# Contrast adjustment of 48 image planes: another cut of the first tile, and the weights by memsets

## The chip, the cores and the metric

One NeuronCore of a Trainium2 chip runs the kernel. The metric is the device time of one execution in microseconds; smaller is better. The other numbers come from one execution that was recorded by the hardware profiler: every instruction with its start and duration on its engine (TensorE is PE, VectorE is DVE, ScalarE is ACT, GpSimd is POOL, SyncE is SP), and every packet that the core's 16 DMA engines moved.

## The reference

```python
def setup_inputs():
    batch, c, h, w = 16, 3, 512, 512
    ...
        "factor": np.float32(1.5),
...
def reference(x: np.ndarray, factor: np.float32) -> np.ndarray:
    mean = np.mean(x, axis=(2, 3), keepdims=True)
    return np.clip(mean + factor * (x - mean), 0, 1).astype(np.float32)
```

There are 16 x 3 = 48 planes of 512 x 512 float32 numbers, 50.33 MB in all. Each plane is pulled away from its own mean by the factor 1.5 and clipped to 0 to 1. A plane can only be written once all of it has been read. All 50.33 MB are read once and written once.

## The kernel before

The numbers are laid out as rows of 16384 (64 KB). A plane is 16 rows; a tile is 128 rows, one per partition, so 8 planes and 8 MB; there are 6 tiles. A ring of three tiles (192 KB in each partition) holds the data. A tile is changed in place and stored from where it was loaded, so the load of tile t + 3 into a slot waits until the same half of tile t has been stored.

SP issues all loads (`load`, line 84) and ACT all stores (`store`, line 87). The two queues share the 16 DMA engines. Each engine executes its own instructions in the order of the program; nothing is reordered.

For every tile, `add` (line 89) makes the row sums: VectorE adds the first columns of each piece (line 94, `tensor_reduce`), and ScalarE the last 3840 (line 98, an activation that copies into `junk` and accumulates). The tile is one piece, except the first and the last, which are added in two halves of 8192 columns. TensorE then multiplies the sums by `blockw` (line 105): a matrix of 128 x 128 with the number (1 - factor) / 262144 where two rows belong to the same plane and zero elsewhere. The result, `shift`, is the mean times (1 - factor), on each row of the plane. `clip` (line 110) makes the output with two VectorE instructions: times the factor plus the shift (line 112), then maximum with 0 and minimum with 1 (line 115).

`blockw` is made by GpSimd (POOL) at the start: a memset (line 66) and two affine selects (lines 68 and 72), which set to zero what lies outside the blocks of 16 x 16 on the diagonal.

Three constants cut the tiles by columns:

```python
FIRST = ((0, 2048), (2048, HALF), (HALF, ROW))
HALVES = ((0, HALF), (HALF, ROW))
WHOLE = ((0, ROW),)
```

In bytes per row FIRST is 8, 24 and 32 KB, that is 1, 3 and 4 MB of a tile. Tile 0 is loaded in two transfers: 8 KB and 56 KB (lines 120 and 121). It is added in halves, and clipped and stored by the three pieces of FIRST, each stored as soon as it is clipped. The other tiles are loaded by halves. Tiles 1 to 3 are clipped whole and stored by halves, tile 4 is clipped and stored whole, tile 5 is clipped and stored half by half. After each tile's stores the loop issues the loads of the tile three further on.

Of the kernel before, what the change touches and what calls it, by code (L numbers as in the profile page):

```python
# [1 line left out]

# [4 lines left out]


P = 128  # L10
ROW = 16384
HALF = ROW // 2
BUFS = 3

ACT = 3840

FIRST = ((0, 2048), (2048, HALF), (HALF, ROW))
HALVES = ((0, HALF), (HALF, ROW))
WHOLE = ((0, ROW),)


@with_exitstack
def kernel(
    ctx: ExitStack,
    tc: tile.TileContext,
    x: bass.AP,
    factor: float,
    out: bass.AP,
):

    nc = tc.nc
    f32 = mybir.dt.float32
    Alu = mybir.AluOpType
    Act = mybir.ActivationFunctionType

    B, C, H, W = x.shape  # L40
    n_img, n_pix = B * C, H * W
    rows = n_pix // ROW
    n_tiles = n_img * rows // P
    assert rows * ROW == n_pix and n_tiles * P == n_img * rows

    factor = float(factor)
    wconst = (1.0 - factor) / float(n_pix)

    x_f = x.rearrange("b c h w -> (b c h w)")
    out_f = out.rearrange("b c h w -> (b c h w)")  # L50

    def dram(ap, t, c0, c1):
        return bass.AP(tensor=ap.tensor, offset=t * P * ROW + c0, ap=[[ROW, P], [1, c1 - c0]])

    consts = ctx.enter_context(tc.tile_pool(name="consts", bufs=1))
    xpool = ctx.enter_context(tc.tile_pool(name="xpool", bufs=1))
    small = ctx.enter_context(tc.tile_pool(name="small", bufs=1))
    psum = ctx.enter_context(tc.tile_pool(name="psum", bufs=1, space=bass.MemoryType.PSUM))

    sums = small.tile([P, 4 * n_tiles], f32, name="sums")  # L60
    junk = small.tile([P, ACT], f32, name="junk")
    bias = psum.tile([P, n_tiles], f32, name="bias")


    blockw = consts.tile([P, P], f32, name="blockw")
    nc.gpsimd.memset(blockw, wconst)  # L66
    v = blockw.rearrange("p (g j) -> p g j", j=rows)
    nc.gpsimd.affine_select(  # L68
        out=v, in_=v, pattern=[[-rows, P // rows], [0, rows]], compare_op=Alu.is_ge,
        fill=0.0, base=0, channel_multiplier=1,  # L70
    )
    nc.gpsimd.affine_select(  # L72
        out=v, in_=v, pattern=[[rows, P // rows], [0, rows]], compare_op=Alu.is_ge,
        fill=0.0, base=rows - 1, channel_multiplier=-1,
    )

    ring = xpool.tile([P, BUFS * ROW], f32, name="ring")

    def cols(t, c0, c1):
        a = t % BUFS * ROW  # L80
        return ring[:, a + c0 : a + c1]

    def load(t, c0, c1):
        nc.sync.dma_start(out=cols(t, c0, c1), in_=dram(x_f, t, c0, c1))  # L84

    def store(t, c0, c1):
        nc.scalar.dma_start(out=dram(out_f, t, c0, c1), in_=cols(t, c0, c1))

    def add(t, pieces):

        parts = []
        for c0, c1 in pieces:
            k = 4 * t + len(parts)
            nc.vector.tensor_reduce(  # L94
                out=sums[:, k : k + 1], in_=cols(t, c0, c1 - ACT), axis=mybir.AxisListType.X,
                op=Alu.add,
            )
            nc.scalar.activation(  # L98
                out=junk, in_=cols(t, c1 - ACT, c1), func=Act.Copy,
                accum_out=sums[:, k + 1 : k + 2],  # L100
            )
            parts = [k + 1, *parts, k]
        shift = bias[:, t : t + 1]
        for i, k in enumerate(parts):
            nc.tensor.matmul(  # L105
                shift, blockw, sums[:, k : k + 1], start=i == 0, stop=i == len(parts) - 1
            )
        return shift

    def clip(t, shift, c0, c1):  # L110
        part = cols(t, c0, c1)
        nc.vector.tensor_scalar(  # L112
            out=part, in0=part, scalar1=factor, scalar2=shift, op0=Alu.mult, op1=Alu.add
        )
        nc.vector.tensor_scalar(  # L115
            out=part, in0=part, scalar1=0.0, scalar2=1.0, op0=Alu.max, op1=Alu.min
        )

    with tc.manual_schedule():
        load(0, *FIRST[0])  # L120
        load(0, FIRST[0][1], ROW)
        for t in range(1, BUFS):
            for c0, c1 in HALVES:
                load(t, c0, c1)
        for t in range(n_tiles):
            last = t == n_tiles - 1
            shift = add(t, HALVES if t == 0 or last else WHOLE)

            pieces = FIRST if t == 0 else WHOLE if t == n_tiles - 2 else HALVES
            if t == 0 or last:  # L130
                for c0, c1 in pieces:
                    clip(t, shift, c0, c1)
                    store(t, c0, c1)
            else:
                clip(t, shift, 0, ROW)
                for c0, c1 in pieces:
                    store(t, c0, c1)
            if t + BUFS < n_tiles:
                for c0, c1 in HALVES:
                    load(t + BUFS, c0, c1)  # L140


# [1 line left out]
_INS = ['x', 'factor']  # L144
_OUTS = [((16, 3, 512, 512), 'float32')]

_NUMBERS = {'factor': 1.5}


# [26 lines left out]
```

## Time and profile before

| what | us |
|---|---|
| median of 3 runs (238.91 to 239.1) | 238.98 |
| the profiled execution | 239.31 |
| its span, first to last instruction | 237.6 |
| VectorE busy | 176.8 |
| ScalarE busy | 29.3 |
| TensorE busy | 8.6 |
| GpSimd busy | 1.1 |
| last load lands | 191.48 |
| issues of the two last stores | 206.07, 214.93 |

The profile's page gives busy times by engine, the DMA engines' share in 40 slices and the two queues (q1 carries the loads, q10 the stores). A window's row has its limits and length, then busy time and number of instructions for TensorE, its weight loads, VectorE, ScalarE and GpSimd, then TensorE's granted clock, the busy share of the DMA engines and the GB/s. A row of the timeline has start, duration, engine, line, operation and shapes; in brackets stand the idle time before it and what ended that. A row of the chain of waits has start, duration and what the time is put down to.

### The profile page before, as it was taken

How to read it: one execution, taken by the hardware profiler on the slowest of the kernel's cores; microseconds unless marked ns; L12 is line 12 of the kernel's file. 1: busy time of each engine (PE TensorE's matmuls, PEld its weight loads, DVE VectorE, ACT ScalarE, POOL GpSimd, SP SyncE). 2: the span in 40 equal slices, each digit the busy share in tenths (PEclk: the TensorE clock that was granted, in tenths of full speed). 3: DMA queues.
4: the chain of work that ended last, by engine and by line, in shares of the span. 5: the costliest groups of instructions: out<-in, count | busy, mean ns of one | idle time of the engine just before them, and what ended most of it. 6: DMA issues, size and time to landing. Idle time of an engine off the chain costs nothing.

```text
span 237.6 us, 220 instructions
## 1 busy us (share of the span) xinstructions
PE 8.6 (4%) x32; PEld 7.7 (3%) x32; DVE 176.8 (74%) x26; ACT 29.3 (12%) x17; POOL 1.1 (0%) x7
## 2 busy tenths in 40 slices
PE   0000020000000000000000000000000011000000
PEld 0000020000000000000000000000000011000000
DVE  0002989999899999899898995299999778991000
ACT  2002900041000050000500000230000550000000
POOL 1000000000000000000000000000000000000000
DMA  8997999999999999999999999999999999899996
GB/s 331 463 463 331 441 441 396 418 400 443 417 476 414 414 419 441 441 436 441 441 441 441 436 408 419 419 441 441 436 441 441 441 441 502 386 397 397 441 441 265
DMA packets 3456, 100.66 MB, mean 424 GB/s; under 512 B 384, under 2 KB 384, under 8 KB 384
## 3 DMA queue, kind: packets, MB, share of 16 engines
q1 hardware_dynamic: 1728, 50.33, 49.6%
q10 hardware_dynamic: 1728, 50.33, 49.1%
HBM read 50.33 MB, written 50.33 MB: 424 GB/s over the span
## 4 chain that ended last, share of the span: by engine, by line
DVE 39%; DMA 34%; another core or an unknown queue 8%; issue 6%; PE 2%; ACT 1%; SPq 0%; DVEq 0%; ACTq 0%
DMA ring<-in_x_dram 19%; DVE sums L94 15%; DVE ring L112 15%; DMA out_dram<-ring 14%; DVE ring L115 9%; PE bias L105 2%; ACT junk L98 1%; SPq L84 0%; DVEq L112 0%; DVEq L94 0%; ACTq L98 0%
## 5 line engine op out<-in xcount | busy, mean ns | idle before, releaser
L94 DVE TENSOR_REDUCE sums<-ring 128x1 f32<-128x4352 f32 (+1 forms) x8 | 71.5, 8949 | 33.2 <-DMA ring<-in_x_dram 33.2
L112 DVE TENSOR_SCALAR ring<-ring,bias 128x16384 f32<-128x16384 f32 (+3 forms) x9 | 53.2, 5911 | 4.6 <-PE bias L105 4.6
L115 DVE TENSOR_SCALAR ring<-ring 128x16384 f32<-128x16384 f32 (+3 forms) x9 | 52.6, 5849 | 0.3
L98 ACT ACTIVATE junk<-ring 128x3840 f32<-128x3840 f32 x8 | 27.2, 3403 | 165.0 <-DMA ring<-in_x_dram 86.5
L105 PE MATMUL bias<-sums,blockw 128*128 128x1 f32 x32 | 8.6, 358 | 188.4 <-ACT junk L98 152.8
L105 PEld LDWEIGHTS bias<-sums,blockw 128*128 128x128 f32 x32 | 7.7, 319 | 189.2 <-ACT junk L98 123.8
L98 ACT ACTIVATION_READ_ACCUMULATOR junk<-ring 128x1 f32 x8 | 1.5, 187 | 0.0
L98 ACT ACT_TABLE_LOAD x1 | 1.3, 1283 | 0.8 <-PEq L157 0.8
L68 POOL TENSOR_SCALAR_AFFINE_SELECT blockw<-blockw 128x128 f32<-128x128 f32 x1 | 0.3, 345 | 0.1
L72 POOL TENSOR_SCALAR_AFFINE_SELECT blockw<-blockw 128x128 f32<-128x128 f32 x1 | 0.3, 339 | 0.1
L66 POOL MEMSET blockw<- 128x128 f32 x1 | 0.2, 206 | 0.3 <-POOLq L157 0.3
L157 POOL MEMSET const-bfloat16-1.0<- 128x1 bf16 x1 | 0.1, 102 | 0.0
L157 POOL MEMSET const-uint8-127<- 128x1 uint8 x1 | 0.1, 102 | 0.0
L157 POOL MEMSET const-float32-0.0<- 128x1 f32 x1 | 0.1, 99 | 0.3 <-issue 0.3
L157 POOL MEMSET const-float32-1.0<- 128x1 f32 x1 | 0.1, 99 | 0.0
## 6 DMA issues: line engine op xcount, KB each, us to landing
ring<-in_x_dram SPq DMA_DIRECT2D x10, 4096.0 KB, 24.8
out_dram<-ring ACTq DMA_DIRECT2D x9, 4096.0 KB, 38.7
ring<-in_x_dram SPq DMA_DIRECT2D x1, 7168.0 KB, 21.0
out_dram<-ring ACTq DMA_DIRECT2D x1, 3072.0 KB, 28.1
ring<-in_x_dram SPq DMA_DIRECT2D x1, 1024.0 KB, 4.5
out_dram<-ring ACTq DMA_DIRECT2D x1, 1024.0 KB, 16.8
out_dram<-ring ACTq DMA_DIRECT2D x1, 33.1
```

The source lines that it names most:

```text
L66: nc.gpsimd.memset(blockw, wconst)
L68: nc.gpsimd.affine_select(out=v, in_=v, pattern=[[-rows, P // rows], [0, rows]], compare_op=Alu.is_ge, fill=0.0, base=0, channel_multiplier=1,
L72: nc.gpsimd.affine_select(out=v, in_=v, pattern=[[rows, P // rows], [0, rows]], compare_op=Alu.is_ge, fill=0.0, base=rows - 1, channel_mul ...
L94: nc.vector.tensor_reduce(out=sums[:, k : k + 1], in_=cols(t, c0, c1 - ACT), axis=mybir.AxisListType.X, op=Alu.add,)
L98: nc.scalar.activation(out=junk, in_=cols(t, c1 - ACT, c1), func=Act.Copy, accum_out=sums[:, k + 1 : k + 2],)
L105: nc.tensor.matmul(shift, blockw, sums[:, k : k + 1], start=i == 0, stop=i == len(parts) - 1)
L112: nc.vector.tensor_scalar(out=part, in0=part, scalar1=factor, scalar2=shift, op0=Alu.mult, op1=Alu.add)
L115: nc.vector.tensor_scalar(out=part, in0=part, scalar1=0.0, scalar2=1.0, op0=Alu.max, op1=Alu.min)
L157: nc = _bacc.Bacc("TRN2", target_bir_lowering=False, num_devices=1)
```

## The change

The first tile is loaded by the three pieces of FIRST (8, 24 and 32 KB per row) instead of by two (8 and 56 KB). It is clipped and stored by halves (32 KB per row) instead of by the three pieces. It is still added in halves.

The weights are made by memsets alone: one over the whole matrix with zero; then, in each band of 32 rows, the second 16 columns of all 32 rows with the weight, the upper 16 rows of these columns with zero again, and the upper left 16 x 16 block with the weight. That makes 13 memsets. The matrix is the same.

```diff
+BAND = 32
...
-    nc.gpsimd.memset(blockw, wconst)
-    v = blockw.rearrange("p (g j) -> p g j", j=rows)
-    nc.gpsimd.affine_select(
-        out=v, in_=v, pattern=[[-rows, P // rows], [0, rows]], compare_op=Alu.is_ge,
-        fill=0.0, base=0, channel_multiplier=1,
-    )
-    nc.gpsimd.affine_select(
-        out=v, in_=v, pattern=[[rows, P // rows], [0, rows]], compare_op=Alu.is_ge,
-        fill=0.0, base=rows - 1, channel_multiplier=-1,
-    )
+    nc.gpsimd.memset(blockw, 0.0)
+    for a in range(0, P, BAND):
+        m = a + rows
+        nc.gpsimd.memset(blockw[a : a + BAND, m : a + BAND], wconst)
+        nc.gpsimd.memset(blockw[a:m, m : a + BAND], 0.0)
+        nc.gpsimd.memset(blockw[a:m, a:m], wconst)
...
-        load(0, *FIRST[0])
-        load(0, FIRST[0][1], ROW)
+        for c0, c1 in FIRST:
+            load(0, c0, c1)
...
-            pieces = FIRST if t == 0 else WHOLE if t == n_tiles - 2 else HALVES
+            pieces = WHOLE if t == n_tiles - 2 else HALVES
```

More of the change, by code (lines that the diff above doesn't have):

```diff
@@ L62 @@
     bias = psum.tile([P, n_tiles], f32, name="bias")
+    assert 2 * rows == BAND
     blockw = consts.tile([P, P], f32, name="blockw")
-    nc.gpsimd.memset(blockw, wconst)
-    v = blockw.rearrange("p (g j) -> p g j", j=rows)
-    nc.gpsimd.affine_select(
-        out=v, in_=v, pattern=[[-rows, P // rows], [0, rows]], compare_op=Alu.is_ge,
-        fill=0.0, base=0, channel_multiplier=1,
-    )
-    nc.gpsimd.affine_select(
-        out=v, in_=v, pattern=[[rows, P // rows], [0, rows]], compare_op=Alu.is_ge,
-        fill=0.0, base=rows - 1, channel_multiplier=-1,
-    )
+    nc.gpsimd.memset(blockw, 0.0)
[4 more added lines that the diff above has]
+        nc.gpsimd.memset(blockw[a:m, a:m], wconst)
     ring = xpool.tile([P, BUFS * ROW], f32, name="ring")
```

## The prediction

> **What bounds the kernel now.** I read the page first: the slices of the DMA engines and the two queues.
>
> ```profile
> span 237.6 us, 220 instructions
> DMA  8997999999999999999999999999999999899996
> q1 hardware_dynamic: 1728, 50.33, 49.6%
> q10 hardware_dynamic: 1728, 50.33, 49.1%
> ```
>
> Queue 1 (SP's loads) and queue 10 (ACT's stores) together hold the 16 DMA engines for 98.7% of the span. VectorE, the busiest compute engine, has 74%. Next the sums over stretches; the last two columns are the DMA share and GB/s (a packet counts where it starts).
>
> ```profile
> 3.00:35.00 32.00, 2.00 (x8) 1.86 (x8) 11.95 (x5) 7.00 (x4) 0.00 (x0) 1.00 1.02 440
> 35.00:42.00 7.00, 0.00 (x0) 0.00 (x0) 6.97 (x3) 0.00 (x0) 0.00 (x0) 1.00 0.96 370
> 69.00:192.00 123.00, 3.52 (x12) 3.01 (x12) 109.78 (x13) 14.43 (x9) 0.00 (x0) 1.00 1.00 431
> 192.00:236.40 44.40, 1.87 (x8) 1.78 (x8) 21.93 (x5) 3.06 (x2) 0.00 (x0) 1.00 0.98 424
> ```
>
> Loads alone (first row), loads beside stores (third) and stores alone (fourth) move at the same rate. Only around 35 to 42 us is less moved. The packet records (one per row of a transfer; a transfer of 128 rows gives each engine 8) say what that is. Packets of 8, 24, 32, 56 and 64 KB take 0.309, 0.912, 1.2135, 2.119 and 2.418 us: per KB nearly the same. So 100.66 MB need 3072 x 1.2135 / 16 = 233.0 us. The first packet starts at 1.80 and the last ends at 236.40, 1.17 before the end. Slow packets add 0.36 us per engine in the first 5 us, 0.70 at 34.8 to 41.3 (32 KB loads of 1.3 to 1.6 us, around the first store) and 0.27 at 50.1 to 52.7 (where the 8 KB store ends and the 24 KB one begins). Semaphore writes add 0.22. The sum 1.80 + 233.0 + 0.36 + 0.97 + 0.22 + 1.17 = 237.5 is the span: the engines never run dry.
>
> The chain of waits blames VectorE (39%) as much as DMA (34%); with the queues full, that is only who released what. For the change, the timeline of the first tile and of the last store, and the end of the chain:
>
> ```profile
> 22.26 3.40 ACT L98 ACTIVATE junk<-ring 128x3840 f32<-128x3840 f32 x1 [20.18 <-DMA ring<-in_x_dram]
> 22.34 9.28 DVE L94 TENSOR_REDUCE sums<-ring 128x1 f32<-128x4352 f32 x2 [22.34 <-DMA ring<-in_x_dram]
> 31.67 0.59 PE L105 MATMUL bias<-sums,blockw 128*128 128x1 f32 x2 [0.83 <-DVE sums L94]
> 32.30 1.29 DVE L112 TENSOR_SCALAR ring<-ring,bias 128x2048 f32<-128x2048 f32 x1 [0.68 <-PE bias L105]
> 34.88 15.93 ACTq L87 DMA_DIRECT2D out_dram<-ring  x3
> 206.07 9.20 ACTq L87 DMA_DIRECT2D out_dram<-ring  x2
> ```
>
> ```profile
> 166.63 24.85 DMA ring<-in_x_dram
> 191.56 3.50 ACT junk L98 x2
> 195.11 1.88 PE bias L105 x8
> 197.09 4.50 DVE ring L112
> 201.61 4.43 DVE ring L115
> ```
>
> Both halves of tile 0 wait for one 7 MB load, and VectorE then adds them one after the other. At the other end the last load lands at 191.48 and the two last stores issue 14.59 and 23.45 us later (206.07, 214.93), while tile 4's store still runs: its last packet ends at 217.04 on the slowest engine. That is 11 us of cover, and the change eats from it.
>
> **The change, part by part.** *Weights.* One memset and two selects end at 1.83 us. Thirteen memsets take, by the nearest rows (99 ns for 128x1, 206 ns for 128x128, 0.06 us between dependent ones), 0.21 + 12 x (0.16 to 0.27) from 0.80: done at 2.9 to 4.2 us. Their reader is TensorE, which will first have a sum at 25.9 (below). Cost nothing; without that cover 1.1 to 2.4 us. Nothing else is queued on POOL.
>
> *Loads.* 1, 3 and 4 MB in place of 1 and 7: one more issue on SP (0.33 to 0.55 us), ahead of all later loads, while the engines already have work; the wait of SP for the first landing (5.28) moves from the sixth load to the seventh, five transfers ahead of need. Per engine 8 x 2.119 = 16.95 us become 8 x (0.912 + 1.2135) = 17.00: +0.05. The first half lands near 12.2, the second as before at 22.2. So one reduction and one activation move under the load: the second reduction ends at 22.34 + 4.68 = 27.02, the clip starts 0.68 later, at 27.70 in place of 32.30.
>
> *Stores.* Per engine 8 x (0.309 + 0.912 + 1.2135) = 19.48 us become 16 x 1.2135 = 19.42: -0.06. Two VectorE instructions and one ACT issue less. The first store now needs a whole half: by the last tile's rows 8.98 us from clip to issue, so 36.68 (1.8 us later than 34.88), the second at 45.54 (50.47 before). The store queue meets a load queue that lasts beyond 57 us, so the engines stay full.
>
> The Trainium skill, "DMA: Bandwidth & Descriptors", section "Anatomy of one DMA — SWDGE (gpsimd) path", fits a fixed cost of about 2.0 us per DMA, mostly completion, which speaks against cutting a load in two. By it the extra load would cost an estimated 2 us and the missing store give as much back; by the packet records neither, since the next transfer's packets follow without a gap.
>
> *What follows from the order.* Queues share an engine packet by packet. Before, 8 and 24 KB stores gave loads of 32 KB most of the time; now stores take every second 32 KB turn, and loads fall behind. Loads alone would end at 1.80 + 0.36 + 8 x (0.309 + 0.912) + 88 x 1.2135 = 118.7. Check with before: stores start at 38.9, 79.8 us of loads are left (65.8 packets), beside them 8 x 0.309 + 8 x 0.912 + 49.8 x 1.2135 = 70.2 of stores, plus 0.97 slow: 189.9, and the last load packet did end at 189.87. After: the first store packet came 4.02 us after its issue, so 36.68 + 4.02 = 40.7; the rest doubles: 40.7 + 2 x 78.0 = 196.7, with slow packets 197.7, landing 1.6 later (189.87 to 191.48): 199.3. Last stores issue at 199.3 + 14.59 = 213.9 and 222.8. They must be on the engines by 217.04 and 226.7. The time from issue to first packet I bound by the two rows that show it: 1.00 (first load, 0.80 to 1.80, empty queues) and 4.02 (first store, behind load packets). I take 1.0, since the load queue is empty then as at the start: margin 2.1 us, no gap. At 4.02 the engines run dry for 0.9. If the first store's packets come 1.4 us earlier (their load packets were slow), the last load lands 1.4 later and the worst gap is 2.3.
>
> The same page, section "Specifications", gives about 0.6 us first-byte latency for transfers from SP and ACT. By it the margin would be 2.5 us; no run here shows 0.6.
>
> VectorE's gain is spent on waiting: it is through tile 1 at 45.5 + 13.2 + 0.7 + 17.5 = 76.9 instead of 81.8, but tile 2 lands at about 82 (75.3 before).
>
> *Slow packets.* Whether they come with the first store, with the step from one packet size to another, or by chance, the trace doesn't say: from -0.97 (all gone) to +0.97 (again at each new border). I take nearly what was: the first store beside loads is still there; -0.1.
>
> **Sum.** +0.05 - 0.06 - 0.1 = -0.1 us. The profiled execution took 239.31 (span 237.57 and 1.74 around it), 0.33 above the median of 238.98; on the median's scale 238.9.
>
> **Rivals.** *Faster: the slow packets go.* They lie just where small stores start and change size, and later borders between 32 KB stores show none. Against it: most of the 0.70 is on loads before any store packet ran. Price -0.97 - 0.01: 238.0.
>
> *Slower: the end runs dry.* Loads lag by 8 us, VectorE can't shorten its 14.6 us after the last landing, and tile 4's store ends before the first half of tile 5 is on the engines. It decides once the issue-to-packet time exceeds 3.1 us with the landing at 199.3, or 1.7 at 200.7. Price 0.9 to 2.3 us: 239.9 to 241.2, middle 240.3. Against it: both steps have to fall on the bad side.
>
> *Slower by new slow packets* at each 32 KB border that meets loads: +0.97, 240.0. The trace has six such borders after 85 us with none.
>
> *The change doesn't do what it says*: if tile 0's first half still waits for the second, the first store issues at 41.3, loads get ahead again, and the time is still 238.9, as transfers hide it.
>
> **How the numbers follow.** Forecast, with the last rival in it: 0.50. Faster: 0.24. Dry end: 0.20. New slow packets: 0.06. The measurement can tell about 0.2% (0.48 us) from no change: forecast within it 0.50, faster 0.24, slower 0.26. The range goes from 237.9 (slow packets gone, 0.1 of spread in the runs) to 240.3, the middle of the dry end.
>
> **What would show it.** Right: the first store issue near 36.7, VectorE idle for 5 to 8 us before tiles 2, 3 and 4, the last load landing near 199, DMA rows at 431 GB/s to the end. Wrong: a gap in the DMA engines after 215 us; a last landing beyond 201; slow packets in number other than now; a first half that doesn't land by 13.

## The result

The changed kernel takes 239.61 us (median of 9 runs, 239.51 to 240.14) against 239.08 us before (median of 9, 238.82 to 239.15): a ratio of 1.0026 with a 95% interval of 1.0017 to 1.0035. That is slower by 0.5 us, a little more than the 0.2% taken as the limit of what can be told. The forecast was no change.

The profiled execution took 239.57 us. Its page, the lines that answer to those of before:

```profile
span 237.8 us, 227 instructions
DMA  7999999999999999999999999999999999989996
q1 hardware_dynamic: 1872, 50.33, 49.9%
q10 hardware_dynamic: 1584, 50.33, 49.0%
```

The two queues still hold the engines, now for 98.9% of the span. The timeline of the changed kernel (start, duration, engine, line, operation, shapes; in brackets the idle time before it and what ended it):

```profile
1.75 0.58 POOL L73 MEMSET blockw<- 16x16 f32 x4
...
12.77 4.69 DVE L93 TENSOR_REDUCE sums<-ring 128x1 f32<-128x4352 f32 x1 [12.77 <-DMA ring<-in_x_dram]
...
22.53 4.68 DVE L93 TENSOR_REDUCE sums<-ring 128x1 f32<-128x4352 f32 x1 [5.07 <-DMA ring<-in_x_dram]
...
26.24 1.84 PE L104 MATMUL bias<-sums,blockw 128*128 128x1 f32 x8 [26.24 <-ACT junk L97]
28.18 4.49 DVE L111 TENSOR_SCALAR ring<-ring,bias 128x8192 f32<-128x8192 f32 x1 [0.97 <-PE bias L104]
...
37.17 9.20 ACTq L86 DMA_DIRECT2D out_dram<-ring  x2
...
83.33 13.22 DVE L93 TENSOR_REDUCE sums<-ring 128x1 f32<-128x12544 f32 x1 [5.96 <-DMA ring<-in_x_dram]
...
122.13 13.22 DVE L93 TENSOR_REDUCE sums<-ring 128x1 f32<-128x12544 f32 x1 [7.35 <-DMA ring<-in_x_dram]
...
215.28 9.20 ACTq L86 DMA_DIRECT2D out_dram<-ring  x2
```

The first half of tile 0 is added under the load of the second, the clip starts at 28.18 instead of 32.30, and the first store issues at 37.17. Then VectorE's gain is gone: it waits 5.96 us for tile 2 and 7.35 for tile 3, since the loads lag. The chain of waits has the last load landing at 200.68 (191.48 before):

```profile
159.53 41.15 DMA ring<-in_x_dram
200.68 0.02 issue
```

None of that costs time. The last packet of tile 4's store ends at 217.22 on the slowest engine, and the store issued at 215.28 has its first packets at 216.56 to 217.22: no gap. What costs time is a stretch of four microseconds just ahead of the first store's packets. One window of the changed kernel and the same of the one before (last two columns: DMA share and GB/s):

```profile
38.50:42.50 4.00, 0.00 (x0) 0.00 (x0) 3.96 (x2) 0.00 (x0) 0.00 (x0) 1.00 1.03 287
```

```profile
38.50:42.50 4.00, 0.00 (x0) 0.00 (x0) 4.00 (x2) 0.00 (x0) 0.00 (x0) 1.00 0.89 354
```

287 GB/s, with the engines fully booked, in place of the 433 of later stretches. (The kernel before lost part of the same in this window and part ahead of it, as its first store's packets begin at 38.9.) The packet records show it packet by packet: each engine has one to three 32 KB loads there that take longer than the usual 1.2135 us, up to 2.8. Because the packets of an engine follow each other without a gap, the records can be sorted into 16 chains, one per engine, and each chain's slow packets summed. The mean over the engines, in us beyond the usual time, then three times in us:

```
                         before   after
slow packets, 0 to 30     0.34     0.45
slow packets, 30 to 60    0.99     1.46
slow packets, after 60    0.03     0.00
an engine's last packet 235.72  236.25
the slowest engine's    236.40  236.58
profiled time           239.31  239.57
```

The engines end 0.53 us later on average, which is the difference of the medians. The two profiles lie only 0.26 apart because the profiled run of before, 239.31, lies near the top of that kernel's runs (95 others, beside the experiments, gave 238.66 to 239.50). One of its engines had two more slow packets than the others (0.61 us at 51.4, 0.48 at 67.7) and ended 0.54 after the next. In all 16 profiles of this study the time is the slowest engine's last packet plus 2.9 to 3.3 us.

### The profile page after: what moved, and what is told of

The parts are those of the page before. It is cut to its first block, busy times and chain, and to the rows that moved or that the text cites. A ratio compares the mean times of both kernels' runs of the same rounds, so it can differ in the third digit from the quotient of the medians.

```text
span 237.8 us, 227 instructions
## 1 busy us (share of the span) xinstructions
PE 8.4 (4%) x32; PEld 7.6 (3%) x32; DVE 176.7 (74%) x24; ACT 29.3 (12%) x17; POOL 1.4 (1%) x17
## 4 chain that ended last, share of the span: by engine, by line
DMA 45%; DVE 37%; another core or an unknown queue 6%; issue 2%; PE 2%; ACT 2%; SPq 0%; ACTq 0%; DVEq 0%
DMA ring<-in_x_dram 26%; DMA out_dram<-ring 19%; DVE ring L111 15%; DVE sums L93 11%; DVE ring L114 11%; PE bias L104 2%; ACT junk L97 2%; SPq L83 0%; ACTq L86 0%; DVEq L111 0%; ACTq L97 0%
## 5 line engine op out<-in xcount | busy, mean ns | idle before, releaser
L111 DVE TENSOR_SCALAR ring<-ring,bias 128x8192 f32<-128x8192 f32 (+1 forms) x8 | 53.0, 6623 | 4.9 <-PE bias L104 4.9
L114 DVE TENSOR_SCALAR ring<-ring 128x8192 f32<-128x8192 f32 (+1 forms) x8 | 52.5, 6560 | 0.3
L73 POOL MEMSET blockw<- 16x16 f32 x4 | 0.4, 104 | 0.2
L74 POOL MEMSET blockw<- 16x16 f32 x4 | 0.4, 104 | 0.0
```

Source lines behind the costliest of these rows:

```text
L73: nc.gpsimd.memset(blockw[a:m, m : a + BAND], 0.0)
L74: nc.gpsimd.memset(blockw[a:m, a:m], wconst)
L111: nc.vector.tensor_scalar(out=part, in0=part, scalar1=factor, scalar2=shift, op0=Alu.mult, op1=Alu.add)
L114: nc.vector.tensor_scalar(out=part, in0=part, scalar1=0.0, scalar2=1.0, op0=Alu.max, op1=Alu.min)
```

## The experiments

Each run is told with its ratio to the kernel before, and with the slow packets between 30 and 60 us of its profile (mean per engine).

**The parts alone.** The weights by memsets alone:

```diff
-    nc.gpsimd.affine_select(
...
+    for a in range(0, P, BAND):
...
```

> The kernel before with the weights by memsets alone. Every theory that puts the loss on the DMA engines expects the time of before (238.9 to 239.2 us), with 0.9 to 1.1 us of slow packets per engine between 30 and 55 us as there. If the memsets themselves cost time, it is near 239.6.

239.0 us, ratio 1.000 (0.9991 to 1.0008); slow packets 0.82. The memsets cost nothing.

The loads alone:

```diff
-        load(0, *FIRST[0])
-        load(0, FIRST[0][1], ROW)
+        for c0, c1 in FIRST:
+            load(0, c0, c1)
```

> The kernel before with the first tile loaded in 8, 24 and 32 KB columns, its stores still 8, 24 and 32 KB. My theory (the loss is slow load packets at the first store, and the rows of that store set how much) expects slow packets as before, 0.7 to 1.0 us per engine, only some 4.6 us earlier, and 238.9 to 239.2 us. The rival that loads fall behind by the earlier start expects 239.4 or more.

Slow packets 0.85, but the times fall into groups: six of twelve at 238.95 to 239.09, six at 239.71 to 240.94; median 239.4, ratio 1.003 (1.0011 to 1.0049). The profile is of a 240.94: fifteen engines end at 235.6 to 235.95, one at 237.87, with slow packets from 80 us on, the largest at 102 and 122 us, most of them near the border between two transfers. So another loss appeared here, which returns below.

The stores by halves alone:

```diff
-            pieces = FIRST if t == 0 else WHOLE if t == n_tiles - 2 else HALVES
+            pieces = WHOLE if t == n_tiles - 2 else HALVES
```

> The kernel before with the first tile stored by halves, loaded in 8 and 56 KB. The theory that the 32 KB rows of the first store make the slow packets expects about 1.4 us of them per engine just after the first store's issue (near 41 us) and a time of 239.4 to 239.8 us. The rival that it is the place of the first store in time (which load it meets) expects less than 1.1 us and 239.0 us.

239.1 us, ratio 1.001 (1.0001 to 1.0019); slow packets 0.76, with the first store at 41.68. The theory that 32 KB rows by themselves set the loss fell. Both together, with the old weights (the edits of the last two diffs):

> The changed kernel with the weights by affine selects as before. Since the memsets alone changed nothing (239.0 us), every theory expects the changed kernel's 239.5 to 239.7 us and about 1.45 us of slow load packets per engine between 38 and 43 us. 239.0 us here would mean that the memsets matter after all, together with the rest.

239.66 us, ratio 1.0025 (1.0014 to 1.0036); slow packets 1.29, first store at 37.25. So the changed kernel's loss comes again from the two edits together; neither alone gave as many slow packets (0.85 and 0.76), and the loads alone had a loss of another kind.

**What kind of start is slow.** The changed kernel with a small store on ACT's queue at the very start:

```diff
+    nc.vector.memset(junk[:, 0:128], 0.0)
...
+        nc.scalar.dma_start(out=dram(out_f, 0, 0, 128), in_=junk[:, 0:128])
```

> The changed kernel with one store more on ACT's queue at the start: 128 rows of 512 bytes of zeros into the first columns of the output, which the real store overwrites later. If the slow packets belong to the first use of ACT's queue, or to the first write to HBM, they go from 38 to 42 us (1.4 us per engine) and at most some of it shows at the start: 238.2 to 238.8 us. If they belong to the first large store beside loads, nothing changes at 38 to 42 us and the time is 239.6 to 239.9 us.

239.79 us, ratio 1.0033 (1.0021 to 1.0044). The slow packets fell to 0.90 but did not go, and 0.2 us came at the start and 0.25 later. A first use of ACT's queue, or a first write, is at most a part. The changed kernel with all transfers on one queue:

```diff
-        nc.scalar.dma_start(out=dram(out_f, t, c0, c1), in_=cols(t, c0, c1))
+        nc.sync.dma_start(out=dram(out_f, t, c0, c1), in_=cols(t, c0, c1))
```

> The changed kernel with every store issued by SP, on the loads' queue, so that loads and stores follow each other in one order and never take turns. If the slow load packets come from two queues taking turns (at the first store and at transfer borders), they go, and the time is 233.0 us of packets + 1.8 + 1.2 + 0.5 at the start + 1.7 outside the span = 238.2 us, below both kernels. If any first store slows the loads around it, 1 us or more of slow packets stays and the time is 239 us or more; a gap in the engines, where SP waits for a landing with nothing queued, would add to it.

240.13 us, ratio 1.005 (1.0038 to 1.0063). There was no gap, and the slow packets stayed: 1.13. Two windows of this run show where they moved:

```profile
38.50:42.50 4.00, 0.00 (x0) 0.00 (x0) 3.96 (x2) 0.39 (x1) 0.00 (x0) 1.00 1.10 475
57.00:61.70 4.70, 0.59 (x2) 0.50 (x2) 3.95 (x2) 0.00 (x0) 0.00 (x0) 1.00 1.00 328
```

The first store issues at 37.24 as in the changed kernel, but its packets stand behind all loads and begin at 61.72; the loads that are slow are those of 57 to 61.7. So in this run it is neither two queues taking turns nor the moment of the issue: the last loads ahead of the first store packets are slow, wherever these come. Nor is it VectorE's clip beside the loads: from 38.5 to 42.5 us VectorE is as busy as in the changed kernel (3.96 us of 4), and the loads move 475 GB/s in place of its 287 (a packet counts where it starts, so that a short window can show more than 433). Of the three later changes from loads to stores two cost this run some 0.2 us more (99 and 177 us), the one at 139 us next to nothing.

**The place in time.** One reduction more on VectorE ahead of the first clip delays the first store and changes nothing else:

```diff
+            if t == 0:
+                nc.vector.tensor_reduce(
+                    out=sums[:, 6:7], in_=cols(0, 0, 5120), axis=mybir.AxisListType.X, op=Alu.add
+                )
```

> The changed kernel with one reduction more on VectorE (5120 columns of tile 0 into an unused column of sums) ahead of the first clip, so that the first store issues near 41.7 us as it did with halves and two loads (0.73 us slow per engine, 239.1 us). If the time at which the first store meets the loads sets the slow packets, they fall to 0.6 to 0.9 us and the time to 239.0 us. If three loads with a first store of 32 KB rows set them, they stay at 1.3 to 1.6 us and the time at 239.6 us. The later store also brings the loads back ahead by some 4 us; if the lag of the loads cost the time, it falls too, but with the slow packets unchanged.

239.25 us, ratio 1.0010 (1.0002 to 1.0019); slow packets 0.92, first store at 41.92. Most of the loss is gone, although VectorE works 5.5 us more. The profiled run itself took 239.65: its engines end at 235.93 on average, but the slowest at 236.66. With 2976 columns:

> The same with 2976 columns: first store near 39.4 us, between the two. By the theory of the place in time the slow packets lie between 0.7 and 1.5 us per engine and the time between 239.0 and 239.6 us; by the theory of the pair 1.3 to 1.6 us and 239.6 us.

242.39 us, ratio 1.0138 (1.0120 to 1.0155): neither theory. The slow packets at the first store are 1.01, but 3.01 us of new ones came after 60. The windows of this run and of the changed kernel:

```profile
60.00:192.00 132.00, 4.11 (x14) 3.51 (x14) 111.22 (x13) 10.49 (x6) 0.00 (x0) 1.00 1.00 424
```

```profile
60.00:192.00 132.00, 3.51 (x12) 3.00 (x12) 109.04 (x11) 10.49 (x6) 0.00 (x0) 1.00 1.00 433
```

424 GB/s against 433 over 132 us. The slow packets are loads and come in clumps, at 62 to 65, 84 to 86, 102 to 105, 122 to 125, 144, 162 to 165 and 183: where one store transfer ends and the next begins, 0.2 to 0.6 us per engine at a time. In this run a store transfer begins about 3 us after a load transfer does (63.6 and 60.4); in the changed kernel they begin together (61.9 and 61.7), in the one delayed to 41.92 they lie 8 us apart (66.2 and 58.5), in the one before 12 (87.9 and 75.5), and none of these has more than 0.10 us of slow packets after 60.

The kernel before was delayed in the same way, with 2784 columns for the place in time alone, and with 5632 to test the reading of the borders:

> The kernel before with such a reduction of 2784 columns, so that its first store (8 KB rows) issues near 37.2 us, where the changed kernel's does. If the place in time alone sets the slow packets, they rise from 0.97 towards 1.45 us per engine and the time to 239.4 to 239.6 us; if it takes the 32 KB rows as well, it stays at 238.9 to 239.1 us.

239.36 us, ratio 1.0011 (1.0002 to 1.0020); slow packets 0.85 and 0.22 later. The place of the changed kernel's first store, with 8 KB rows, does not give its 1.46. The times do not decide: six of the eleven, from 239.36 up, lie near the changed kernel's, the other five (238.74 to 239.15) with the kernel before.

> The kernel before with a reduction of 5632 columns ahead of the first clip, so that its first store issues near 40.5 us. The theory that loss at the later borders depends on how far a store transfer's border lies behind a load transfer's border: the run with 2976 columns lost 0.5 us per border at 3 us behind; here the same 3 us behind should come out, with slow load packets at most borders after 70 us and 241 us or more. If that loss belongs to the three loads and halves, this one stays at 239.0 to 239.7 us.

241.28 us, ratio 1.0107 (1.0092 to 1.0123), as forecast; but the profile is of the quickest of its five (239.83; slow packets 0.79), without the clumps.

> The kernel before with a reduction of 5632 columns once more, for another profile: four of its five unprofiled or profiled times were 240.7 to 241.7 us, but the profile on hand is of its quick one (239.8 us). If the borders of the two queues make the loss, a profile of 241 us shows slow load packets of 0.3 to 0.7 us at most store borders after 70 us; if it is something else, they lie elsewhere or the engines have gaps.

238.88 us in this one run, slow packets 0.91, again without clumps. In both profiles a store transfer begins 3 to 4 us after a load transfer only early on (56.2 and 53.3, 57.7 and 53.7); from 126 us on it begins 12 us after (126.6 and 114.5). So the two profiles do not hold the condition that was to be tested at the later borders. The same program gave 239.83 to 241.65 in one set of runs and 238.88 in another, so the border reading rests on the run with 2976 columns and on the one engine of the loads-alone run; what makes a run fall into it is open. The changed kernel with 9088 columns:

> The changed kernel with a reduction of 9088 columns ahead of the first clip: first store near 46 us, so that its first packets meet the next border between two load transfers (near 51 us), one transfer later than the changed kernel's own meet theirs (42.5 us). If 32 KB store rows that begin at a border of the load queue are what costs, the slow packets are again 1.2 to 1.5 us per engine, with none at the later borders, and the time is 239.5 to 239.8 us. If it is something about 42 us alone, they are 0.7 to 1.0 us and the time is 239.0 to 239.3 us.

239.19 us, ratio 1.0007 (0.9998 to 1.0016): no loss that can be told. Its profile is of its slowest run (239.57), with 1.1 us of slow packets ahead of the first store's packets (issue 45.62, first packet 50.93) and 0.3 at 36 to 42: 1.44 in all, as the theory of the border expects, while the times are those of its rival. By the times a border of the load queue does not make the loss; one profile of an untypical run can't settle it.

Two more, after the cause was narrowed to the slow packets. The first leaves the second half of tile 0 out of its mean:

```diff
-            shift = add(t, HALVES if t == 0 or last else WHOLE)
+            shift = add(t, HALVES[:1] if t == 0 else HALVES if last else WHOLE)
...
+                    out=sums[:, 6:7], in_=cols(0, 0, 5312), axis=mybir.AxisListType.X, op=Alu.add
```

> The changed kernel with the second half of tile 0 left out of its mean, and a reduction of 5312 columns ahead of the first clip, so that the first store issues near 32.4 us instead of 37.2. By the rule of turns the last load then lands near 205 us and the first store of tile 5 issues near 220 us, after tile 4's store has ended at 217: a gap of 3 to 5 us in the engines and 242.5 to 244.5 us. The slow packets at the first store (33 to 38 us) are 1.3 us or more per engine if they grow the earlier it comes, 0.7 to 1.1 if 37.2 us is a place by itself.

239.03 us, ratio 1.0002 (0.9993 to 1.0012); slow packets 0.99, first store at 32.32. The gap at the end did not come, because the last load landed at 195.4 and not at 205. The timeline says why:

```profile
80.52 0.82 ACTq L86 DMA_DIRECT2D out_dram<-ring  x2
...
195.38 4.69 DVE L93 TENSOR_REDUCE sums<-ring 128x1 f32<-128x4352 f32 x1 [2.62 <-DMA ring<-in_x_dram]
...
209.95 9.20 ACTq L86 DMA_DIRECT2D out_dram<-ring  x2
```

Tile 1's stores issue at 80.52 and have their first packets at 84.3, but tile 0's had run out at 75.2: for 9 us the loads had the engines to themselves. Loads cannot lag without bound, since stores are made of what has been loaded. The last run cut the first store's rows to 16 KB:

```diff
+FIRST16 = ((0, 4096), (4096, HALF), (HALF, ROW))
...
-            pieces = WHOLE if t == n_tiles - 2 else HALVES
+            pieces = FIRST16 if t == 0 else WHOLE if t == n_tiles - 2 else HALVES
...
+                    out=sums[:, 6:7], in_=cols(0, 0, 4880), axis=mybir.AxisListType.X, op=Alu.add
```

> The changed kernel with the first half of tile 0 clipped and stored in two pieces of 16 KB rows, and a reduction of 4880 columns ahead, so that the first store issues near 37.2 us with rows of half the size. If the row size sets the loss at this place, the slow packets from 38 to 43 us lie between those of 8 KB rows (0.4 us) and 32 KB rows (1.3 to 1.45): 0.7 to 1.0 us per engine. If the place alone does, 1.3 us or more.

239.65 us, ratio 1.0029 (1.0018 to 1.0040), as slow as the changed kernel. The profile, with 0.91 of slow packets, is of the quickest of its nine runs (239.28) and so cannot say what the others had: inconclusive on the row size.

**What follows.** By the times, a first store at 37.2 us behind the three loads costs 0.5 to 0.6 us whether its rows have 32 KB (239.61, 239.66) or 16 KB (239.65); at 32.3, 41.9 and 45.6 us, in otherwise like kernels, it costs 0 to 0.25 (239.03, 239.25, 239.19), and at 39.4 us 3.4 (242.39), most of it at later borders. By the profiles, one for each kernel, the cost is slow load packets, between 30 and 60 us in all 16 profiles, 0.76 to 1.46 us per engine: nearly all ahead of the first store's packets where that store has 16 or 32 KB rows, and in part where the 24 KB store begins where it has 8. Why the loads are slow there, and why most at that place, is not settled. No version was faster than the kernel before.

## Why the prediction was wrong

- *The bound, right.* The engines have no gap from the first to the last packet in either kernel, and the kernel's time follows the packets. That my sum for before met the span is partly luck: it adds the mean of the slow packets and comes to the end of the slowest engine (236.40), while the engines end at 235.72 on average. The 0.6 between is in the records of successive packets, which overlap by some 3 ns each (on the mean 16.05 packets run at a time on the 16 engines).
- *Weights, right in cost.* They end at 2.33 us, sooner than forecast (2.9 to 4.2), and alone they change nothing.
- *First tile, right but for 0.5 us.* The first half landed at 12.67 (12.2), the second at 22.51 (22.2). The clip started at 28.18, not 27.70: I put TensorE's tail at the 0.68 us that followed VectorE's last sum before, but all eight matmuls now wait for ScalarE's last sum (26.1) and take 1.84 us. The first store issued at 37.17 (36.68).
- *Turns, right.* The Trainium skill, "DMA: Bandwidth & Descriptors", section "Queues, rings and completion order", has each engine alternate between queues packet by packet. The forecast landing by that was 199.3, measured 200.68; the last stores issued at 215.28 and 224.14 (213.9 and 222.8), and VectorE waited 5 to 8 us as forecast. The last load packet did end at 197.90 (197.7 forecast); what I had wrong is the 1.6 us from there to the landing. The 4-byte packet that closes a load takes its own turn: before, it came on the last engine 1.20 us after the last row (189.87), behind one 32 KB store row; after, 2.41 us after it, behind one 64 KB row of tile 4's store. The early-store run shows where my use of the rule ends: loads take twice their time only while the store queue is supplied.
- *Dry end, rightly not forecast.* The first engine had a packet of the new store 1.28 us after the issue, so 1.28 at most is the time that I bounded by 1.00 and 4.02, and took at 1.0. The margin was there, though with the later landing only 1.7 us would have fitted.
- *A transfer more or less, right.* +0.05 and -0.06 us, and no fixed cost per transfer, in chains without gaps.
- *Slow packets, the step that failed.* "I take nearly what was: the first store beside loads is still there; -0.1." The mechanism was named, its size was not: 1.46 instead of 0.99 between 30 and 60 us, +0.47, and +0.11 at the start, where the sum had -0.1 for all of it. Together that is the 0.53 by which the engines end later, within 0.05. Why these packets grew stays open. The upper bound, +0.97, held it. But I gave that side 0.06, as slow packets at each later border of 32 KB stores, and looked for them where before had none; they came at the one border that before did show. Two rows of one profile (0.70 at the first store, 0.27 at the second) can't tell how far such a term moves with the place of the store, and a term of 0.4% with an unknown cause should not have left half of the chance to a limit of 0.2%.
- *The base.* 239.31 was taken as 0.33 above the median and scaled; the packet records show why: one late engine.

## What to carry to other kernels

With the DMA engines full, work that VectorE finished earlier was worth nothing here. What is left are the packets that take longer than their size: sort the packet records into one chain per engine, sum what lies above the usual time, and look at the slowest engine's end. Such losses depend on when a store meets the loads: a shift by 2.3 us cost 1.2% here (239.61 to 242.39). So with a change that shifts the first store, run it with two or three delays as well, before the time is put down to the change itself.

## What had not been expected of the hardware

Loads just ahead of the first store packets took up to 2.8 us instead of 1.2135, and up to 2.35 with one queue for both. The closing packet of a load waited behind one row of the other queue, 1.20 or 2.41 us by that row's size. A store delayed by 2.3 us lost another 3.0 us per engine at later transfer borders, with 424 GB/s instead of 433 between 60 and 192 us. And a single engine with slow packets is enough to make the kernel later by almost 2 us (237.87 against 235.95 for the next).
